# Second feed-forward matmul by half-block products: four of eight hidden groups with seven products instead of eight, in two passes

## The chip, the cores and the metric

The kernel runs on one core of one Trainium2 chip. The metric is device time in microseconds (us) of one execution; the times below are medians of several runs. Engines are named as in the profile: PE is TensorE's matmul (PEld its weight load), DVE is VectorE, ACT is ScalarE, POOL is GpSimd, SP issues the DMAs.

## The reference, cut to what matters

One layer of a streaming encoder on a sequence of 512 frames with 1024 channels. The change touches the last part of it alone, the second matmul of the feed-forward block:

```python
xn = modulate(rmsnorm(h, norm2_g[l]), sh2, sc2)
ff = jnp.square(jax.nn.relu(xn @ w_ff1[l])) @ w_ff2[l]     # (512 x 4096) @ (4096 x 1024)
h = h + g2[:, None, :] * ff
...
return rmsnorm(h, final_g)
```

All of it is float32 to about float32's precision. A matmul is made of three: each operand is split into a high part (rounded to the matmul's own 32-bit form, fp32r) and the low rest, and high x high, low x high and high x low are summed in PSUM (`mm3`, lines 116 to 119).

## The kernel before, in words

The first feed-forward matmul (w_ff1) computes the 4096 hidden channels in eight groups of 512, groups 1 to 7 by seven half-block products P1 to P7 instead of eight, so that scheme is already in use there (lines 1010 to 1030; its products are the rows named P). The squared-relu results stay in SBUF as sixteen tiles `hq[n, nh, th]` for group n: half nh of the group's 512 hidden channels, half th of the 512 frames, 128 x 512 elements each. Rows name them h.

The second matmul (w_ff2) then runs over 32 pieces k of 128 hidden rows. A piece is loaded on SP's queue (`raw_f`, 512 KB), ACT rounds it to its high part (`wh_f`, line 95), DVE subtracts to get the low part (`wl_f`, line 96); the hidden tiles are split in the same way on DVE (`hsh`, `hsl`, lines 1040 and 1041). Each piece is 24 matmuls of 128x128 by 128x512: four blocks of frames, two halves of the 1024 columns, three matmuls each, into eight PSUM banks `ob`. Up to three pieces are split ahead (the pools `raws` and `wpool` have three buffers each). The last four pieces (`LAST`) are split early and multiplied block by block, so that the gate, residual and final norm of one block run while the next is multiplied.

Each engine runs its instructions in the order in which they stand in the program, which a scheduler has set; a waiting instruction holds up all behind it on that engine. Tiles of a closed pool give their memory to the next pool, and what is written there waits for the last reader of the old tile.

Of the kernel before, what the change touches and what calls it, by code (L numbers as in the profile page):

```python
# [49 lines left out]
def block_kernel(ctx, tc, vecs_d, rows_d, ws_d, x_d, w_ada, w_in, w_out, w_ff1, w_ff2, out_d):  # L50
    nc = tc.nc
    act, dve, pool, pe, sp = nc.scalar, nc.vector, nc.gpsimd, nc.tensor, nc.sync

# [705 lines left out]
    for half in range(2):  # L759
        cs = slice(half * 512, (half + 1) * 512)  # L760
# [6 lines left out]
        for k in range(4 * half, 4 * half + 4):  # L767
# [75 lines left out]
    for k in range(KT):  # L843
# [169 lines left out]
    for n in range(1, NB):  # L1013
        c = {(nh, th): ring(f"h{n}{nh}{th}") for nh in range(2) for th in range(2)}
# [17 lines left out]
    ws_ff = Stream([(w_ff2[k * P:(k + 1) * P, :], 1, D, f"f2{k}") for k in range(FF // P - LAST)], 2)  # L1032
    ws_ff.prefetch(2)
    hsq = {}

    def hs_pair(kp, alloc):
        for th in range(2):
            src = hq[kp // 2, kp % 2, th]
            h_, l_ = alloc(th)
            dve.tensor_copy(out=h_, in_=src)  # L1040
            dve.tensor_sub(out=l_, in0=src, in1=h_.bitcast(F32))  # L1041
            hsq[kp, th] = (h_, l_)

    def hs_sc(th):
        hl = fp.tile([P, 2, 2, 256], F32R, tag="sc", name=f"hs0{th}", bufs=2)
        return hl[:, 0], hl[:, 1]

    hs_pair(0, hs_sc)
# [6 lines left out]
    o_banks = [[bank(f"ob{t}{hf}") for hf in range(2)] for t in range(TB)]  # L1055
    NK = FF // P

    def ff2_piece(k, last=False):
        if last:
            raw = raws.tile([P, 1, D], F32, tag="raw", name=f"raw_f2{k}")  # L1060
            sp.dma_start(out=raw[:, 0, :], in_=w_ff2[k * P:(k + 1) * P, :])
            wh = hsp.tile([P, 1, D], F32R, tag="lwh", name=f"wh_f2{k}", bufs=LAST)
# [5 lines left out]
        if k % 2 == 0 and k > 0:  # L1068
            hs_pair(k // 2, lambda th: [hsp.tile([P, 2, 256], F32R, tag="hs" + q, name=f"hs{q}{k}{th}", bufs=4)
                                        for q in "hl"])  # L1070
        return wh, wl

    def mm_f2(k, t, hf, wh, wl, stop):
        cs = slice(hf * 512, (hf + 1) * 512)
        h_, l_ = (v[:, k % 2, (t % 2) * P:(t % 2 + 1) * P] for v in hsq[k // 2, t // 2])
        mm3(o_banks[t][hf], h_, l_, wh[:, 0, cs], wl[:, 0, cs], k == 0, stop)

    for k in range(NK - LAST):
        wh, wl = ff2_piece(k)
# [80 lines left out]
```

## Time and profile before

| | |
|---|---|
| median of 3 runs | 819.65 us (819.43 to 820.51) |
| the profiled execution: its time, its span | 822.66 us, 820.1 us |
| PE busy in the span | 807.5 us (98%) |
| DVE, ACT busy | 554.4 us (68%), 359.4 us (44%) |
| second feed-forward matmul | about 637 to 812 us of the span |
| read from HBM | 104.44 MB |

Busy is the share of the span in which an engine had an instruction in work. The span is that of the profiled execution; its time is 2.6 us longer, and the runs without the profiler have a median 3.0 us below it. The page's second section has the granted clock of TensorE in tenths; it is at 9 in all slices of the second matmul.

### The profile page before, as it was taken

To read this page: it belongs to the slowest core of one execution; us is meant where nothing else is said; L and a number is where in the kernel's file an instruction comes from. 1 tells how busy PE (TensorE), PEld (TensorE's weight loads), DVE (VectorE), ACT (ScalarE), POOL (GpSimd) and SP (SyncE) were. 2 spreads that over 40 slices of the span, in tenths; PEclk is the share of its full clock that TensorE was granted. 3 is DMA by queue.
4 is the path that set the end of the run, shared out by engine and by line. 5 is a ranking of instruction groups with operands and counts; after the bars stand their busy time and mean duration, and the time that the engine had idled before them with its cause. 6 is when DMAs were issued, how large, how long until landed. Compare 5 with 4: busy or idle time off the path is not lost.

```text
span 820.1 us, 11377 instructions
## 1 busy us (share of the span) xinstructions
PE 807.5 (98%) x4423; PEld 700.8 (85%) x4423; DVE 554.4 (68%) x863; ACT 359.4 (44%) x540; POOL 43.1 (5%) x62
## 2 busy tenths in 40 slices
PE   8999999999999999999999999999999999999995
PEld 6887888888888888888888899999999888888884
DVE  4889767684834367988666689888888544444555
ACT  5457556274432333232444456666666311222213
POOL 2004020121100000100000000000000000000000
PEclk8999999999999999999999999999999999999998
DMA  8974331153233399577344241333321433223402
GB/s 254 268 229 119 116 104 47 27 136 96 78 103 94 110 330 293 169 247 271 108 170 159 83 126 51 104 106 109 116 83 54 152 103 103 83 98 103 129 0 103
DMA packets 66823, 107.28 MB, mean 131 GB/s; under 512 B 5329, under 2 KB 38225, under 8 KB 66769
## 3 DMA queue, kind: packets, MB, share of 16 engines
q1 hardware_dynamic: 66768, 106.56, 41.6%
q8 instruction: 34, 0.56, 0.3%
q14 instruction: 21, 0.16, 0.1%
HBM read 104.44 MB, written 2.10 MB: 130 GB/s over the span
## 4 chain that ended last, share of the span: by engine, by line
PE 93%; ACT 2%; DMA 1%; DVE 1%; issue 1%; POOL 0%; SPq 0%; POOLq 0%; DVEq 0%
PE ob L119 7%; PE ob L118 7%; PE ob L117 7%; PE P L118 6%; PE P L119 6%; PE P L117 6%; PE qk L282 4%; PE wo L117 1%; PE wo L119 1%; PE wo L118 1%; PE cp L241 1%; PE k1b L117 1%; PE gb0b L118 1%; PE q1b L118 1%; PE q1b L119 1%
## 5 line engine op out<-in xcount | busy, mean ns | idle before, releaser
L117 PE MATMUL ob<-wh_f,hsh 128*128 128x512 f32 x240 | 93.4, 389 | 0.0
L118 PE MATMUL ob<-wl_f,hsh 128*128 128x512 f32 x240 | 93.4, 389 | 0.0
L119 PE MATMUL ob<-wh_f,hsl 128*128 128x512 f32 x240 | 93.4, 389 | 0.0
L95 ACT CAST wh_f<-raw_f 128x1024 fp32r<-128x1024 f32 x28 | 29.6, 1056 | 110.6 <-PE ob L119 107.6
L96 DVE TENSOR_TENSOR wl_f<-raw_f,wh_f 128x1024 fp32r<-128x1024 f32 x28 | 34.3, 1225 | 55.7 <-ACT wh_f L95 54.7
L117 PEld LDWEIGHTS ob<-wh_f,hsh 128*128 128x128 f32 x240 | 45.1, 188 | 9.4
L118 PEld LDWEIGHTS ob<-wl_f,hsh 128*128 128x128 f32 x240 | 45.1, 188 | 9.4
L119 PEld LDWEIGHTS ob<-wh_f,hsl 128*128 128x128 f32 x240 | 45.1, 188 | 9.2
L921 ACT CAST wh_T<-T 128x1024 fp32r<-128x1024 f32 x21 | 22.0, 1049 | 22.8 <-PE P L118 21.1
L117 PE MATMUL P<-x2h,wh_B 128*128 128x256 f32 x112 | 31.6, 282 | 0.0
L118 PE MATMUL P<-x2l,wh_B 128*128 128x256 f32 x112 | 31.6, 282 | 0.0
L119 PE MATMUL P<-x2h,wl_B 128*128 128x256 f32 x112 | 31.6, 282 | 0.0
L1040 DVE CAST hsh<-h 128x512 fp32r<-128x512 f32 x30 | 12.7, 425 | 25.5 <-PE ob L118 25.5
L921 ACT CAST wh_B<-B 128x1024 fp32r<-128x1024 f32 x21 | 22.0, 1049 | 16.7 <-PE P L118 15.7
L922 DVE TENSOR_TENSOR wl_T<-T,wh_T 128x1024 fp32r<-128x1024 f32 x21 | 25.7, 1224 | 2.5 <-ACT wh_T L921 2.5
L922 DVE TENSOR_TENSOR wl_B<-B,wh_B 128x1024 fp32r<-128x1024 f32 x21 | 25.6, 1218 | 0.1
L96 DVE TENSOR_TENSOR wl_gb<-raw_gb,wh_gb 128x1024 fp32r<-128x1024 f32 x8 | 9.8, 1224 | 19.7 <-ACT wh_gb L95 19.6
L1041 DVE TENSOR_TENSOR hsl<-h,hsh 128x512 fp32r<-128x512 f32 x30 | 20.7, 692 | 2.6
L667 DVE SCALAR_TENSOR_TENSOR accg<-arg,c_act,accg 128x1024 f32<-128x1024 f32 x14 | 18.0, 1283 | 6.3 <-DMA arg<-in_w_ada 6.1
L118 PEld LDWEIGHTS P<-x2l,wh_B 128*128 128x128 f32 x112 | 21.3, 190 | 0.0
L117 PEld LDWEIGHTS P<-x2h,wh_B 128*128 128x128 f32 x112 | 21.3, 190 | 0.0
L119 PEld LDWEIGHTS P<-x2h,wl_B 128*128 128x128 f32 x112 | 21.3, 190 | 0.0
(548 smaller groups left out, 2491.8 us busy)
## 6 DMA issues: line engine op xcount, KB each, us to landing
raw_f<-in_w_ff SPq DMA_DIRECT2D x36, 512.0 KB, 3.3
B<-in_w_ff SPq DMA_DIRECT2D x28, 512.0 KB, 3.8
ar<-in_w_ada SPq DMA_DIRECT2D x64, 128.0 KB, 3.3
arg<-in_w_ada SPq DMA_DIRECT2D x16, 512.0 KB, 6.0
raw_o<-in_w_in SPq DMA_DIRECT2D x8, 512.0 KB, 3.8
raw_mv<-in_w_in SPq DMA_DIRECT2D x8, 512.0 KB, 3.6
raw_gb<-in_w_in SPq DMA_DIRECT2D x8, 512.0 KB, 3.7
raw_v<-in_w_in SPq DMA_DIRECT2D x8, 512.0 KB, 3.6
```

The source lines that it names most:

```text
L95: act.copy(out=wh, in_=raw)
L96: dve.tensor_sub(out=wl, in0=raw, in1=wh.bitcast(F32))
L117: pe.matmul(out, lhsT=ah, rhs=bh, start=start, stop=False)
L118: pe.matmul(out, lhsT=ah, rhs=bl, start=False, stop=False)
L119: pe.matmul(out, lhsT=al, rhs=bh, start=False, stop=stop)
L241: pe.matmul(cps[c][:, o:o + 1], lhsT=tile_[:, vi, f * P:(f + 1) * P], rhs=rhs, start=first and q == 0, stop=last and q == len(todo) - 1)
L282: pe.matmul(bk, lhsT=wx[:, kk, f * P:(f + 1) * P], rhs=xx[k], start=k == 0 and ps_ == 0, stop=k == KT - 1 and ps_ == 2)
L667: dve.scalar_tensor_tensor(out=acc, in0=raw, scalar=c_act[:, k:k + 1], in1=acc, op0=ALU.mult, op1=ALU.add)
L921: act.copy(out=wh, in_=src)
L922: dve.tensor_sub(out=wl, in0=src, in1=wh.bitcast(F32))
L1040: dve.tensor_copy(out=h_, in_=src)
L1041: dve.tensor_sub(out=l_, in0=src, in1=h_.bitcast(F32))
```

## The change

Of the eight hidden groups, six are done in a new way before the last two. A group of 512 hidden rows is a product of the 512 x 512 hidden values, in halves by frames and by hidden channels (a11, a12 for the first half of the frames, a21, a22 for the second), with 512 rows of w_ff2, in halves by rows and by columns (F11, F12, F21, F22 in the load's names, 512 KB each). A step is one product of half-blocks: 12 matmuls of 128x128 by 128x512 into two banks.

Groups 0, 1, 3 and 4 (W) take seven steps: P1 = a11 F11, P2 = a12 F21, P7 = (a11 - a21)(F22 - F12), P3 = (a12 - a21 - a22 + a11) F22, P5 = (a21 + a22)(F12 - F11), P6 = (a21 + a22 - a11)(F22 - F12 + F11) and P4 = a22 (F21 - F22 + F12 - F11). Groups 2 and 5 (S) take the plain eight steps, named P2, P3 (first pass) and P4, E (second pass). All groups add into the same banks g..., so eight banks would not hold seven products of two banks: the first pass runs P1, P2, P7, P3 over groups 0 to 5, the second P5, P6, P4 (and E) over the same groups with the weights loaded again. Between and after the passes DVE combines the banks into tiles r. Groups 6 and 7 (pieces k = 24 to 31) follow as before, and continue in the banks of P4 and E for the second half of the frames.

```diff
+    GROUPS = "WWSWWS"
...
+    left = Feed({0: (0, "F11"), 1: (0, "F21")}, order,
+                lambda nm: raws.tile([P, 2, 512], F32, tag="raw", name=nm), 3)
+    right = Feed({0: (1, "F12"), 1: (1, "F22")}, order,
+                 lambda nm: pass_pool[0].tile([P, 2, 512], F32, tag="q2", name=nm, bufs=4), 0)
...
+        if i % 5 < 3:
+            wh, wl = wtile("wh", f"wh_g{i}", 2, 512), wtile("wl", f"wl_g{i}", 2, 512)
+        else:
+            wh, wl = (pass_pool[0].tile([P, 2, 512], F32R, tag="wx" + q, name=f"w{q}_x{i}", bufs=2) for q in "hl")
+        act.copy(out=wh, in_=src)
+        dve.tensor_sub(out=wl, in0=src, in1=wh.bitcast(F32))
...
+        act.copy(out=h_, in_=src)
+        dve.tensor_sub(out=l_, in0=src, in1=h_.bitcast(F32))
...
+                if kind == "W" and pas == 0:
+                    yield hl(a11), w_pair(left.get(), left)
+                    yield hl(a12), w_pair(left.get(), left)
+                    b12, b22 = right.get(), right.get()
+                    s3 = fp.tile([P, 2, 256], F32, tag="tmp", name=f"S3{n}", bufs=2)
+                    dve.tensor_sub(out=s3, in0=a11, in1=a21)
+                    dve.tensor_sub(out=b12, in0=b22, in1=b12)
+                    yield hl(s3), w_pair(b12, right)
+                    dve.tensor_add(out=a21, in0=a21, in1=a22)
+                    dve.tensor_sub(out=a11, in0=a21, in1=a11)
+                    dve.tensor_sub(out=a12, in0=a12, in1=a11)
+                    yield hl(a12), w_pair(b22, right)
+                elif kind == "W":
+                    b11, b12 = left.get(), right.get()
+                    dve.tensor_sub(out=b12, in0=b12, in1=b11)
...
+                    yield hl(a21), w_pair(b12)
+                    b22 = right.get()
+                    dve.tensor_sub(out=b22, in0=b22, in1=b12)
...
+                    yield hl(a11), w_pair(b22)
+                    b21 = left.get()
+                    dve.tensor_sub(out=b21, in0=b21, in1=b22)
...
+                    yield hl(a22), w_pair(b21, left)
...
     x2s.close()
     mhs.close()
     hsp = ff.enter_context(tc.tile_pool(name="hsp", bufs=1, side="right"))
     fing = hsp.tile([P, D], F32, name="fing")
     sp.dma_start(out=fing, in_=rows_d[5].partition_broadcast(P))
+    ps_stack = ExitStack()
+    pass_pool.append(ps_stack.enter_context(tc.tile_pool(name="passes", bufs=1, side="right")))
+    for _ in range(4):
+        right.more()
...
+    for i, (pas, key) in enumerate(plan_):
+        prefetch_step(5)
+        (h_, l_), (wh, wl) = ready.pop(0)
...
+            for j in range(2):
+                mm3(acc_b[key, t], h_[:, j, ts_], l_[:, j, ts_], wh[:, j], wl[:, j], first and j == 0,
+                    i == last_of[key] and j == 1 and key not in ("P4", "E"))
...
+    ps_stack.close()
+    lwp = ff.enter_context(tc.tile_pool(name="lwp", bufs=1, side="right"))
```

The buffers of F12 and F22 (`q2`) and two of the five pairs of split weights (`wx`) lie in a pool on the memory that the first matmul's operands held; F11 and F21 use the buffers that `raw_f` had.

On SP's queue, where the first matmul ends (B are its last loads, raw_f the pieces of w_ff2, fing the final norm's row), there stood before:

```order
L916 DMA B710_5909<-in_w_ff1 128x4x256
L93 DMA raw_f20_6231<-in_w_ff2 128x1024
L916 DMA B711_5911<-in_w_ff1 128x4x256
L93 DMA raw_f21_6237<-in_w_ff2 128x1024
L93 DMA raw_f22_6264<-in_w_ff2 128x1024
```

Now there stands, from the second of the B loads on:

```order
L916 DMA B711_5911<-in_w_ff1 128x4x256
L1053 DMA F21022_6233<-in_w_ff2 128x2x512
L1053 DMA F11121_6235<-in_w_ff2 128x2x512
L1053 DMA F21120_6244<-in_w_ff2 128x2x512
L1053 DMA F12023_6265<-in_w_ff2 128x2x512
L1053 DMA F11219_6253<-in_w_ff2 128x2x512
L1147 DMA fing_6260<-in_rows 128x1024
L1053 DMA F22022_6267<-in_w_ff2 128x2x512
L1053 DMA F12121_6269<-in_w_ff2 128x2x512
L1053 DMA F22120_6271<-in_w_ff2 128x2x512
```

The third digit of an F name is its group: F22 of group 0 (F22022), the second load into the new pool, stands behind fing and a load for group 2.

On DVE around the last addition of the first matmul, h710 (h are hidden tiles, S and F sums and weights, hsl and wl the low parts), there stood before:

```order
L96 TENSOR_TENSOR wl_f20_6234<-raw_f20_6231,wh_f20_6233 128x1024
L1027 TENSOR_TENSOR h701_6015<-h701_6015,P47_6175 128x512
L96 TENSOR_TENSOR wl_f21_6240<-raw_f21_6237,wh_f21_6239 128x1024
L1029 TENSOR_TENSOR h710_6016<-h710_6016,P37_6203 128x512
L1040 CAST hsh20_6330<-h010_4529 128x512
L96 TENSOR_TENSOR wl_f22_6267<-raw_f22_6264,wh_f22_6266 128x1024
```

and now, seven operations behind h710:

```order
L1093 TENSOR_TENSOR hsl7_6351<-S31_6347,hsh7_6350 128x512
L1109 TENSOR_TENSOR h100_4596<-h101_4597,h100_4596 128x512
L1105 TENSOR_TENSOR S34_6619<-h400_5307,h401_5308 128x512
L1110 TENSOR_TENSOR h110_4598<-h110_4598,h100_4596 128x512
L1106 TENSOR_TENSOR F12023_6265<-F22022_6267,F12023_6265 128x1024
L1076 TENSOR_TENSOR wl_x3_6294<-F22022_6267,wh_x3_6293 128x1024
L1076 TENSOR_TENSOR wl_x4_6304<-F11121_6235,wh_x4_6303 128x1024
L1076 TENSOR_TENSOR wl_g2_6281<-F12023_6265,wh_g2_6280 128x1024
```

Behind h710 the next weight's split stood second before. Now ten operations of 128x512 stand there (the last four of them are shown), and F12023, the first that needs F22022, stands eleventh.

On PE the first 24 matmuls of the second matmul were those of piece 0, and piece 1 followed (ob are the banks, wh_f20 and wh_f21 the high parts of the two pieces):

```order
L119 MATMUL ob30_6262<-wh_f20_6233,hs01_6246 128x512
L117 MATMUL ob31_6263<-wh_f20_6233,hs01_6246 128x512
L118 MATMUL ob31_6263<-wl_f20_6234,hs01_6246 128x512
L119 MATMUL ob31_6263<-wh_f20_6233,hs01_6246 128x512
L117 MATMUL ob00_6256<-wh_f21_6239,hs00_6243 128x512
L118 MATMUL ob00_6256<-wl_f21_6240,hs00_6243 128x512
```

Now P1 and P2 of group 0 take the place of piece 0, and from the last matmul of P2 on there stands (gP1, gP2, gP3, gP7 are the banks; wh_g2 is the high part of F22 - F12, wh_x3 of F22, wh_x4 of the next group's F11):

```order
L119 MATMUL gP21_6340<-wh_g1_6249,hs01_6246 128x512
L117 MATMUL gP10_6309<-wh_x4_6303,hsh5_6299 128x512
L117 MATMUL gP11_6316<-wh_x4_6303,hsh5_6299 128x512
L117 MATMUL gP70_6360<-wh_g2_6280,hsh3_6276 128x512
L117 MATMUL gP71_6367<-wh_g2_6280,hsh3_6276 128x512
L117 MATMUL gP30_6387<-wh_x3_6293,hsh4_6289 128x512
L118 MATMUL gP30_6387<-wl_x3_6294,hsh4_6289 128x512
L119 MATMUL gP30_6387<-wh_x3_6293,hsl4_6290 128x512
L117 MATMUL gP30_6387<-wh_x3_6293,hsh4_6289 128x512
L118 MATMUL gP30_6387<-wl_x3_6294,hsh4_6289 128x512
L119 MATMUL gP30_6387<-wh_x3_6293,hsl4_6290 128x512
L118 MATMUL gP70_6360<-wl_g2_6281,hsh3_6276 128x512
```

Two matmuls of group 1 were put ahead of P7 and P3 of group 0; P7's low part, wl_g2, is wanted eight matmuls after P7's first. In all PE has 4295 rows in place of 4343.

## Rows read from the trace of the kernel before

**Rows 1.** The page: the span, its first section (busy us, share, instructions), and the head of the chain that ended last, by engine.

```profile
span 820.1 us, 11377 instructions
PE 807.5 (98%) x4423; PEld 700.8 (85%) x4423; DVE 554.4 (68%) x863; ACT 359.4 (44%) x540; POOL 43.1 (5%) x62
PE 93%; ACT 2%; DMA 1%; DVE 1%; issue 1%; POOL 0%; SPq 0%; POOLq 0%; DVEq 0%
```

**Rows 2.** All waits of PE in the whole span, by what it waited for: us in total, times, longest us.

```profile
PE xt L321 <- POOL epsc L307: 2.5, 1, 2.5
PE xt L315 <- DVE xt L333: 1.3, 2, 0.8
PE k1b L117 <- ACT wh_k L95: 0.2, 1, 0.2
```

**Rows 3.** Busy us (and instructions) of each engine in stretches, granted clock, DMA share, GB/s: one of the first matmul's, its crossing to the second, one of the second.

```profile
600.00:620.00 20.00, 20.00 (x171) 20.00 (x171) 17.34 (x19) 12.91 (x17) 0.00 (x0) 1.00 0.25 79
637.00:660.00 23.00, 23.00 (x106) 19.12 (x105) 11.17 (x18) 5.93 (x7) 0.00 (x0) 1.00 0.43 138
660.00:700.00 40.00, 40.00 (x178) 33.15 (x177) 16.96 (x21) 7.89 (x8) 0.00 (x0) 1.00 0.28 93
```

**Rows 4.** The matmuls of the second matmul: duration ns min/median/max, first and last start us. The first row is of pieces 0 and 1, the other of the rest.

```profile
L117 PE MATMUL ob<-wh_f,hs x16: 389/389/396, 637.5 to 647.7; 128*128 128x512 f32 x16
L119 PE MATMUL ob<-wh_f,hsl x240: 388/389/389, 648.8 to 811.3; 128*128 128x512 f32 x120
```

**Rows 5.** PE in order of time at the crossing: start us, us, instruction.

```profile
637.34 0.28 PE L119 MATMUL P<-S4hl,wl_B 128*128 128x256 f32 x1
637.46 0.40 PE L117 MATMUL ob<-wh_f,hs 128*128 128x512 f32 x1
```

**Rows 6.** DVE in order of time, in the first matmul and at its crossing to the second (in brackets: idle before it, what ended that).

```profile
522.18 1.23 DVE L922 TENSOR_TENSOR wl_T<-B,wh_T 128x1024 fp32r<-128x1024 f32 x1 [1.46 <-ACT wh_T L921]
570.65 1.22 DVE L922 TENSOR_TENSOR wl_B<-B,wh_B 128x1024 fp32r<-128x1024 f32 x1
571.78 1.22 DVE L943 TENSOR_TENSOR T<-B,T 128x1024 f32<-128x1024 f32 x1
572.92 0.68 DVE L1024 TENSOR_TENSOR h<-h,P 128x512 f32<-128x512 f32 x1
573.52 0.68 DVE L1025 TENSOR_TENSOR h<-h,P 128x512 f32<-128x512 f32 x1
574.12 1.22 DVE L922 TENSOR_TENSOR wl_B<-B,wh_B 128x1024 fp32r<-128x1024 f32 x1
637.66 0.69 DVE L1029 TENSOR_TENSOR h<-h,P 128x512 f32<-128x512 f32 x1 [0.65 <-PE P L119]
649.65 1.23 DVE L96 TENSOR_TENSOR wl_f<-raw_f,wh_f 128x1024 fp32r<-128x1024 f32 x1 [4.21 <-ACT wh_f L95]
```

**Rows 7.** ACT in order of time: a 128x512 cast with what follows it, and 128x1024 casts at the crossing.

```profile
497.41 0.62 ACT L989 CAST S1hl<-xn 128x512 fp32r<-128x512 f32 x1
497.93 0.59 ACT L976 ACTIVATE h<-f10b 128x512 f32<-128x512 f32 x1
634.70 1.05 ACT L95 CAST wh_f<-raw_f 128x1024 fp32r<-128x1024 f32 x1 [0.59 <-PE P L118]
635.65 0.63 ACT L976 ACTIVATE h<-h 128x512 f32<-128x512 f32 x1
```

**Rows 8.** SP's queue at the crossing in order of time, and from the page the DMA issues (KB each, median us to landing).

```profile
634.43 2.94 SPq L93 DMA_DIRECT2D raw_f<-in_w_ff  x2
637.65 0.67 SPq L1053 DMA_DIRECT2D fing<-in_rows  x1
639.87 5.92 SPq L93 DMA_DIRECT2D raw_f<-in_w_ff  x2
...
fing<-in_rows SPq DMA_DIRECT2D x1, 512.0 KB, 5.7
```

**Rows 9.** The same table for the six microseconds after the crossing and two of the single ones in them (last two columns: DMA share, GB/s), and for one loaded stretch.

```profile
638.00:644.00 6.00, 6.00 (x28) 4.98 (x27) 5.35 (x10) 2.63 (x4) 0.00 (x0) 1.00 0.80 261
641.00:642.00 1.00, 1.00 (x6) 0.83 (x5) 1.00 (x3) 0.00 (x0) 0.00 (x0) 1.00 0.74 201
643.00:644.00 1.00, 1.00 (x6) 0.84 (x5) 0.38 (x1) 0.88 (x1) 0.00 (x0) 1.00 0.28 115
290.00:295.00 5.00, 5.00 (x24) 4.14 (x23) 1.43 (x2) 1.06 (x1) 0.52 (x1) 1.00 1.00 374
```

**Rows 10.** The granted clock (third column from the right, 1.00 is 2.4 GHz, 0.50 is 1.2 GHz) at the start of the kernel and after its last matmul, as stretches.

```profile
14.00:15.00 1.00, 1.00 (x12) 1.00 (x10) 0.96 (x3) 0.74 (x2) 0.00 (x0) 0.98 0.88 165
15.00:18.30 3.30, 3.30 (x14) 3.01 (x14) 2.27 (x9) 2.10 (x4) 0.00 (x0) 0.50 0.90 254
18.30:21.80 3.50, 3.50 (x10) 2.73 (x9) 3.43 (x12) 2.15 (x6) 0.00 (x0) 0.50 0.92 272
21.80:23.00 1.20, 1.20 (x8) 1.01 (x8) 0.84 (x2) 1.18 (x3) 0.00 (x0) 1.00 0.88 247
...
811.00:812.00 1.00, 0.73 (x4) 0.26 (x2) 0.43 (x2) 0.30 (x2) 0.00 (x0) 1.00 1.03 383
813.50:813.75 0.25, 0.00 (x0) 0.00 (x0) 0.25 (x1) 0.25 (x1) 0.00 (x0) 0.86 0.00 0
813.75:814.00 0.25, 0.00 (x0) 0.00 (x0) 0.19 (x2) 0.19 (x2) 0.00 (x0) 0.50 0.00 0
```

More of the change, by code (lines that the diff above doesn't have):

```diff
@@ L1030, in block_kernel @@
         relu2(c12, c12)
[L1032 to L1046, printed above, removed]
@@ L1048, in block_kernel, with later, __init__, more @@
-    hs_pair(0, hs_sc)
+    GROUPS = "WWSWWS"
+    NF = len(GROUPS)
+    NK = FF // P
+    KF = 4 * NF
+    def later(kind, pas):
+        return {("W", 0): ("P1", "P2", "P7", "P3"), ("W", 1): ("P5", "P6", "P4"),
+                ("S", 0): ("P2", "P3", "P2", "P3"), ("S", 1): ("P4", "E", "P4", "E")}[kind, pas]
+    class Feed:
+        def __init__(self, cols, order, make, ahead):
+            self.todo = [(n, kh, cols[kh]) for n in order for kh in range(2)]
+            self.make, self.have = make, []
+            for _ in range(ahead):
+                self.more()
+        def more(self):
+            if self.todo:
+                n, kh, (jh, nm) = self.todo.pop(0)
+                raw = self.make(f"{nm}{n}{len(self.todo)}")
+                r0 = n * 512 + kh_rows[nm] * 256
+                sp.dma_start(out=raw, in_=w_ff2[r0:r0 + 256, jh * 512:(jh + 1) * 512].rearrange("(k p) c -> p k c", p=P))
+                self.have.append(raw)
+        def get(self):
+            return self.have.pop(0)
@@ new lines, in block_kernel, with w_pair @@
+    kh_rows = {"F11": 0, "F21": 1, "F12": 0, "F22": 1}
+    order = list(range(NF)) * 2
+    left = Feed({0: (0, "F11"), 1: (0, "F21")}, order,
+                lambda nm: raws.tile([P, 2, 512], F32, tag="raw", name=nm), 3)
+    right = Feed({0: (1, "F12"), 1: (1, "F22")}, order,
+                 lambda nm: pass_pool[0].tile([P, 2, 512], F32, tag="q2", name=nm, bufs=4), 0)
+    pass_pool = []
+    count = [0, 0]
+    def w_pair(src, feed=None):
+        i = count[0]
+        count[0] += 1
+        if i % 5 < 3:
[4 more added lines that the diff above has]
+        dve.tensor_sub(out=wl, in0=src, in1=wh.bitcast(F32))
+        if feed:
+            feed.more()
+        return wh, wl
@@ L1049, in block_kernel, with prefetch_step @@
+    plan_ = [(pas, key) for pas in range(2) for kind in GROUPS for key in later(kind, pas)]
+    gen = passes()
+    ready = []
+    def prefetch_step(m):
+        while len(ready) < m:
+            s_ = next(gen, None)
+            if s_ is None:
+                return
+            ready.append(s_)
+    prefetch_step(2)
     x2s.close()
@@ new lines, in block_kernel, with rtile, gated, after @@
+    acc_b, res = {}, {}
+    def rtile(nm, t):
+        res[nm, t] = hsp.tile([P, 512], F32, name=f"r{nm}{t}")
+        return res[nm, t]
+    def gated(nm, t, row, hf):
+        cs = slice(hf * 512, (hf + 1) * 512)
+        r_ = res[nm, t]
+        dve.tensor_mul(out=r_, in0=r_, in1=g2[:, cs])
+        dve.tensor_add(out=xr[:, row, cs], in0=xr[:, row, cs], in1=r_)
+    def after(key):
+        for t in range(2):
+            b_ = acc_b.get((key, t))
+            if key == "P1":
+                act.copy(out=rtile("1", t), in_=b_)
+            elif key == "P7":
+                dve.tensor_add(out=rtile("7", t), in0=res["1", t], in1=b_)
+            elif key == "P3":
+                dve.tensor_add(out=rtile("3", t), in0=res["1", t], in1=b_)
+            elif key == "P2":
+                dve.tensor_add(out=res["1", t], in0=res["1", t], in1=b_)
+            elif key == "P6":
+                dve.tensor_add(out=res["3", t], in0=res["3", t], in1=b_)
+                dve.tensor_add(out=res["7", t], in0=res["7", t], in1=b_)
+            elif key == "P5":
+                dve.tensor_add(out=res["3", t], in0=res["3", t], in1=b_)
+                dve.tensor_add(out=rtile("5", t), in0=res["7", t], in1=b_)
@@ L1058, in ff2_piece @@
+    ps_stack.close()
+    lwp = ff.enter_context(tc.tile_pool(name="lwp", bufs=1, side="right"))
+    o_banks = [[bank(f"ob{t}{hf}") for hf in range(2)] for t in range(2)]
+    o_banks += [[acc_b["P4", t], acc_b["E", t]] for t in range(2)]
+    late = [(nm, t, row + t, hf) for nm, row, hf in (("3", 0, 1), ("7", 2, 0), ("5", 2, 1)) for t in range(2)]
     def ff2_piece(k, last=False):
@@ L1067, in ff2_piece @@
             wh, wl = ws_ff.next()
-        if k % 2 == 0 and k > 0:
-            hs_pair(k // 2, lambda th: [hsp.tile([P, 2, 256], F32R, tag="hs" + q, name=f"hs{q}{k}{th}", bufs=4)
-                                        for q in "hl"])
+        if k % 2 == 0 and k > KF:
+            hs_pair(k // 2)
         return wh, wl
@@ L1075, in mm_f2 @@
         h_, l_ = (v[:, k % 2, (t % 2) * P:(t % 2 + 1) * P] for v in hsq[k // 2, t // 2])
-        mm3(o_banks[t][hf], h_, l_, wh[:, 0, cs], wl[:, 0, cs], k == 0, stop)
-    for k in range(NK - LAST):
+        mm3(o_banks[t][hf], h_, l_, wh[:, 0, cs], wl[:, 0, cs], k == KF and t < 2, stop)
+    for k in range(KF, NK - LAST):
         wh, wl = ff2_piece(k)
@@ L1082, in block_kernel @@
                 mm_f2(k, t, hf, wh, wl, False)
+        for _ in range(2):
+            if late:
+                gated(*late.pop(0))
     pcs = [ff2_piece(k, True) for k in range(NK - LAST, NK)]
```

55 lines of the change are left out of this document (51 added, 4 removed).

## The prediction

> **What bounds the kernel now.** I read the page first: PE is busy for 98% of the span, and the chain that ended last is PE for 93% [rows 1]. Then the waits of PE: three rows in all, each of transposes or of an early projection, and none that names a weight or a hidden tile of the feed-forward block [rows 2]. So the second feed-forward matmul is PE at its own pace. Its 768 matmuls (32 pieces of 24) start between 637.46 us and 811.3 us [rows 4, 5], 173.8 us over 767 steps, 0.2267 us each (the 389 ns of a row [rows 4] overlap one another). Last, the stretch table, for what could take PE's place: DVE is busy for 16.96 of 40 us in the second matmul, ACT for 7.89, DMA for a share of 0.28, all at full clock [rows 3]. In the first matmul, which already uses seven products, DVE stands at 17.34 of 20 us and PE still doesn't wait [rows 3].
>
> **What the change removes.** Four groups go from 8 to 7 steps of 12 matmuls: 48 matmuls less, the same number by which the order of PE shrinks. 48 × 0.2267 = 10.88 us. A step lasts 12 × 0.2267 = 2.72 us, so four steps 10.88 us and the three steps of a W group in the second pass 8.16 us.
>
> **What it adds on DVE and ACT, pass by pass.** Behind each other, DVE operations start 1.13 us apart at 128x1024 (570.65, 571.78, 572.92) and 0.60 us apart at 128x512, operands in PSUM included (572.92, 573.52, 574.12) [rows 6]; I use 1.135 and 0.60. W in the first pass: four weight splits and a weight sum (5 × 1.135), four hidden splits and four hidden sums (8 × 0.60), 10.5 us of 10.88. W in the second pass: three splits and three sums of weights, three hidden splits, 6 × 1.135 + 3 × 0.60 = 8.6 us of 8.16, so 0.45 short. S: 4 × 1.135 + 2 × 0.60 = 5.7 us of 10.88, 5.1 to spare. ACT needs 0.95 + 0.52 us per step [rows 7], 1.5 of 2.72. The folds between the passes put eight additions (4.8 us) on DVE within the first two W groups of the second pass, so DVE falls behind there by up to 4.8 + 2 × 0.45 = 5.7 us. What hides it is the lead: there are five pairs of split weights, so DVE can be four steps (10.9 us) ahead, less a cast and a split (2.1 us), 8.8. The S group that follows gives 5.1 us back, the next two W groups take 0.9, and the last folds (eight additions) fall in the second S. I put this at **0**; without the lead it would cost the 5.7. Groups 6 and 7 have twelve additions and multiplications for the gates, 7.2 us, in 16 steps of which DVE now uses 42% [rows 3]: also 0. A few sums for group 0 and later move ahead into the first matmul; DVE has gaps there such as the 1.46 us at 522 us [rows 6], and I put 0.1 us for one that meets none; at most two operations, 1.2 us.
>
> **What it adds on the queue.** Groups 0 to 5 are loaded twice, 24 loads of 0.524 MB more. The first pass needs 2.1 MB per 10.88 us (193 GB/s), a W group of the second 2.1 MB per 8.16 us (257 GB/s). The kernel has moved 374 GB/s over 5 us [rows 9]. I put the loads at **0**; the other bound is a rival below.
>
> **The entry, where a new wait stands.** PE does P1 and P2 of group 0 from 637.46, 24 × 0.2267, and is through at 642.9. Next it wants F22 − F12 of group 0. F22 lies in the new pool, whose memory comes free with the last product of the first matmul at 637.3 to 637.7 [rows 5]. On SP it stands behind a load for group 2 and fing: of the two loads at 634.43 that took 2.94 us to issue the second leaves at about 637.1, fing at 637.65 with 0.67 [rows 8], so F22 is issued at about 638.3. How long it is under way: fing, the same size beside others, took 5.7 us [rows 8], and the 6 us from 638 moved 1.57 MB (261 GB/s), three loads, with the rate falling from 201 to 115 by 643 [rows 9], so three are in at about 643.5. I take 643.8 (642.5 to 646). Meanwhile DVE does ten half operations behind h710, which starts at 637.66 with 0.69 [rows 6]: 638.35 + 10 × 0.60 = 644.35. Then the weight sum (645.5). ACT casts wh_x3, wh_x4 and wh_g2 in this order, 0.95 apart [rows 7]: the third follows the sum and is there at 646.85. PE has only the two matmuls of P1 of group 1 between (0.45 us, at about 645.9, when wh_x4 is there). So it goes on at 646.9: 646.9 − 642.9 − 0.45 = 3.55 us lost. Eight matmuls on (648.7) it wants wl_g2; DVE has wl_x3 and wl_x4 before it, 1.135 each, and ends wl_g2 at 648.9: 0.2 more. Together **3.8 us**. An earlier load doesn't help by more than 0.2, since DVE isn't free before 644.35; a load that lands at 646 makes it 5.8. Everything behind on PE simply moves by this amount.
>
> **What the stall does to the clock.** From about 643.1 (the last matmul's end) to 645.9 PE has no matmul, 2.8 us, then two, then 0.6 us none. After the kernel's last matmul, ended at 811.73, the granted clock held 1.00 at first and was at 0.50 by 813.75, in a slice that averages 0.86 [rows 10]: it fell at 813.7, 2.0 us after PE fell idle. By that row it falls to half (1.2 GHz) here too, before the matmuls come back. How long it then stays isn't shown for a gap in the middle; the nearest rows are the start, 0.50 from 15.0 to 21.8 with few matmuls [rows 10]. At half the clock each us costs half a us. The bounds are 0 and 6.8 / 2 = 3.4; I take the middle, **1.7 us**, since PE is fully loaded at once when it comes back, where at the start it was not. The Trainium skill, "TensorE: Matmul & The Clock Gate", section "HAM oscillation — how this bites in real kernels", tells of kernels whose matmuls wait for a DMA between bursts and come back at the half clock; it speaks against this change, the trace shows no such gap in the second matmul, and the fall at 813.7 agrees with it. By it the sum below is −5.3, and if it didn't hold for one gap of this length, −7.0.
>
> **The sum.** −10.88 + 0.1 + 3.8 + 1.7 = −5.3 us on the profiled span, 820.1 to 814.8. The profiled execution took 822.66 us, the runs' median is 819.65, 3.0 below; the same step from the median gives **814.4 us**. The stretch behind the last matmul I leave as it is.
>
> **Rivals.** *The clock holds through the gap.* The row at 811 to 814 speaks against it, the two matmuls in the middle of the gap for it. −7.0 us, 812.6.
> *DVE becomes the bound in the second pass.* If its operations there don't overlap each other's ends but take their full 1.23 and 0.69 us [rows 6], a W group takes 6 × 1.23 + 3 × 0.69 = 9.45 us against 8.16: four groups fall 5.2 short and the eight fold additions 5.5 more; of these the S between gives back some 4.6 and the lead covers the rest only in part, as it is itself smaller after the entry. About 5 us: 819.3, no change that could be measured. Against it: the first matmul runs DVE at 87% with no wait of PE [rows 2, 3].
> *The loads bind; slower than before.* The first pass draws 193 GB/s and the second 257 GB/s in its W groups, each with at most seven loads ahead, whose buffers come free late. For it: the stretch at the entry reached only 261 GB/s with three loads in flight [rows 9], and two issues of loads take 2.94 us of SP [rows 8], about 1.5 each, so that four per W group take 6 of 8.16 us. Against it: 374 GB/s with more in flight [rows 9]. The saving left, 5.3 us, is gone when the four W groups of the second pass take 8.16 + 5.3 / 4 = 9.5 us each, 221 GB/s; at 200 GB/s they take 10.5 us, 9.4 us in all, and the time is 823.8.
> That the products stay as many is no rival: PE's order has the 48 less.
>
> **How the numbers follow.** The forecast 0.50, the clock that holds 0.28, DVE as bound 0.13, the loads 0.09. The first two span 811.6 (the clock holds, and a us less at the entry if some of the ten half operations are earlier) to 816.5 (the load lands at 646). The range reaches to DVE's case and leaves the loads out: 811.6 to 819.0. A difference of 0.2% (1.6 us) is about what a measurement of this kernel can tell from no change. Faster by more than that, below 818.0: the first two cases and a part of DVE's, 0.82. Same: most of DVE's and a piece of the loads', 0.10. Slower, above 821.3: 0.08.
>
> **What the profile after would show.** PE with 720 matmuls in the second matmul, 0.2267 us apart but for one gap; a wait at about 643 of some 3.5 us that names wh_x4 or wh_g2 (ACT) or F12023's sum, and a short one on wl_g2; the granted clock at 0.50 for some us behind it. DVE at 85 to 90% between 650 and 760 us with no other wait of PE, DMA at 190 to 260 GB/s. Wrong it would be if waits on wl or wh of the second pass stand in PE's list (DVE), if these end with DMAs of F tiles (loads), if the entry's wait is under 2 or over 6 us, or if matmuls in the middle of the passes stand further apart than 0.2267 us.

## The result and the profile after

The changed kernel takes 815.73 us (median; 813.60 to 816.33) against 819.54 us before: a ratio of 0.9941, 95% interval 0.9926 to 0.9956. It is 3.8 us faster by the medians; the forecast was 814.4, 5.3 us less than before. The profiled execution took 815.62 us with a span of 813.8.

The page's first rows, to be read beside [rows 1], and all waits of PE, beside [rows 2] (us in total, times, longest):

```profile
span 813.8 us, 11472 instructions
PE 795.4 (98%) x4375; PEld 689.1 (85%) x4375; DVE 615.3 (76%) x925; ACT 404.1 (50%) x606; POOL 43.0 (5%) x62
PE 93%; DMA 2%; SPq 1%; ACT 1%; issue 1%; DVE 1%; POOLq 0%; POOL 0%
...
PE gP L117 <- ACT wh_x L1075: 4.8, 1, 4.8
PE xt L321 <- POOL epsc L307: 2.5, 1, 2.5
PE xt L315 <- DVE xt L333: 2.3, 2, 1.5
PE gates L288 <- ACT xs L366: 0.7, 1, 0.7
PE qk L282 <- ACT xs L369: 0.3, 1, 0.3
PE k1b L117 <- ACT wh_k L95: 0.2, 1, 0.2
PE gP L117 <- ACT wh_g L1075: 0.2, 1, 0.2
```

There are 48 matmuls less. Two waits are new in the second matmul (the rows of gP), both at its entry, and none stands in the two passes behind it. The waits on gates and qk and the longer one on xt lie in the first 60 us of the span, which the change doesn't touch; the first two are missing again in other runs below (e1 to e8). PE around the entry, in order of time (start us, us; x2 is two matmuls joined in one row; in brackets the idle time before and what ended it), and the kernel's last matmul:

```profile
636.16 0.40 PE L117 MATMUL gP<-wh_g,hs 128*128 128x512 f32 x1
...
641.40 0.39 PE L119 MATMUL gP<-wh_g,hs 128*128 128x512 f32 x1
646.55 0.77 PE L117 MATMUL gP<-wh_x,hsh 128*128 128x512 f32 x2 [4.76 <-ACT wh_x L1075]
647.50 1.22 PE L117 MATMUL gP<-wh_g,hsh 128*128 128x512 f32 x2 [0.17 <-ACT wh_g L1075]
648.52 0.63 PE L117 MATMUL gP<-wh_x,hsh 128*128 128x512 f32 x1
...
650.60 0.40 PE L119 MATMUL gP<-wh_x,hsl 128*128 128x512 f32 x1
...
806.10 0.39 PE L119 MATMUL gE<-wh_f,hsl 128*128 128x512 f32 x1
```

From the first start to the last, 169.94 us go by; 719 steps of 0.2267 are 163.0. So 6.9 us are lost, all of it between 641.40 and 650.60. Two parts of it can be told apart. P2 is through at 641.63, two matmuls of the next group take 0.45, and P7's first starts at 647.50 instead of 642.08: 5.4 us of waiting. From there to 650.60 seven steps take 3.1 us in place of 1.6: 1.5 us of low clock. The second matmul is thus 10.88 - 6.94 = 3.94 us shorter than the 173.88 us of before [rows 4, 5], as the medians say (3.8). The forecast for it was -10.88 + 3.8 + 1.7 = -5.4 us.

The two spans differ by more, 6.3 us. The rest lies where the change has no part: the second matmul starts 1.3 us earlier (636.16 against 637.46 [rows 5]), and behind its last start stand 7.7 us instead of 8.7, though the kernel's last operations of ACT and DVE start 3.45 us behind it in both. Among all the profiled executions here that first start lies anywhere from 635.17 to 637.46. So kernels are compared below by the length of the second matmul from first to last start, less 0.2267 us per step; that is called the loss.

What ended the wait, on DVE, ACT and SP in order of time, and fing's transfer (KB, us from issue to landing):

```profile
642.44 0.69 DVE L1110 TENSOR_TENSOR h<-h,h 128x512 f32<-128x512 f32 x1
644.58 1.22 DVE L1106 TENSOR_TENSOR F<-F,F 128x1024 f32<-128x1024 f32 x1 [1.45 <-DMA F<-in_w_ff]
...
644.51 1.99 ACT L1075 CAST wh_x<-F 128x1024 fp32r<-128x1024 f32 x2 [4.39 <-DMA F<-in_w_ff]
646.41 1.99 ACT L1075 CAST wh_g<-F 128x1024 fp32r<-128x1024 f32 x2
...
636.36 0.84 SPq L1147 DMA_DIRECT2D fing<-in_rows  x1
637.25 0.94 SPq L1053 DMA_DIRECT2D F<-in_w_ff  x2
...
fing<-in_rows SPq DMA_DIRECT2D x1, 512.0 KB, 6.8
```

One load ahead of these, F12 of group 0 (its issue, and us from issue to landing):

```profile
L1053 SPq DMA_DIRECT2D F<-in_w_ff x1: 368/368/368, 633.9 to 633.9; - x1
DMA to landing us min/median/max: 5.3/5.3/5.3
```

PE's list names ACT, but ACT itself and DVE had been idle for 4.39 and 1.45 us, and a DMA ended both: F22 of group 0, issued at 637.25, lands at 644.5. fing lands at 636.36 + 6.8 = 643.2, so F22 comes 1.3 us behind it. F12 lands at 639.2 and the load for group 2, issued at 635.74, at 640.5. Of these issues fing's waits 0.2 us for the first matmul's last product on PE; F22's waits for nothing, SP only reaches it behind fing.

The clock at its fall and its rise (third column from the right), and PE (first after the length), DVE (third) and the GB/s (last) in the two passes, beside [rows 3]:

```profile
646.80:647.00 0.20, 0.20 (x2) 0.05 (x1) 0.20 (x2) 0.20 (x1) 0.00 (x0) 1.00 0.00 0
647.00:647.20 0.20, 0.20 (x2) 0.00 (x0) 0.20 (x1) 0.20 (x1) 0.00 (x0) 0.77 0.00 0
650.40:650.60 0.20, 0.20 (x2) 0.16 (x1) 0.20 (x1) 0.00 (x0) 0.00 (x0) 0.69 0.69 205
650.60:650.80 0.20, 0.20 (x2) 0.19 (x1) 0.20 (x1) 0.00 (x0) 0.00 (x0) 1.00 1.07 317
...
660.00:700.00 40.00, 40.00 (x178) 33.14 (x177) 35.17 (x40) 23.17 (x30) 0.00 (x0) 1.00 0.64 210
700.00:740.00 40.00, 40.00 (x178) 33.12 (x177) 38.60 (x45) 21.56 (x26) 0.00 (x0) 1.00 0.69 219
```

The clock was at 0.50 (1.2 GHz) from 647.1 to 650.5, 3.4 us. This is one execution: its mean granted clock is 0.994, that of the three other runs 0.990, so more of their time stood at 0.50; where is not recorded. (In the kernel before, the last slice of the clock on the page, which reaches into the second matmul, reads 8 and not 9; that is the fall at 813.7, behind the last matmul [rows 10].) In the passes DVE went from 42% to 88% and 96%, and PE keeps its 178 matmuls per 40 us, as many as before.

### The profile page after: what moved, and what is told of

It is laid out like the page before. It is cut to its first block, busy times and chain, and to the rows that moved or that the text cites. A ratio compares the mean times of both kernels' runs of the same rounds, so it can differ in the third digit from the quotient of the medians.

```text
span 813.8 us, 11472 instructions
## 1 busy us (share of the span) xinstructions
PE 795.4 (98%) x4375; PEld 689.1 (85%) x4375; DVE 615.3 (76%) x925; ACT 404.1 (50%) x606; POOL 43.0 (5%) x62
## 4 chain that ended last, share of the span: by engine, by line
PE 93%; DMA 2%; SPq 1%; ACT 1%; issue 1%; DVE 1%; POOLq 0%; POOL 0%
PE P L119 6%; PE P L117 6%; PE P L118 6%; PE gP L117 5%; PE gP L118 5%; PE gP L119 5%; PE qk L282 4%; PE wo L117 2%; PE wo L119 2%; PE wo L118 2%; PE f10b L118 1%; PE f10b L117 1%; PE f10b L119 1%; PE k1b L117 1%; PE o0b L119 1%
## 5 line engine op out<-in xcount | busy, mean ns | idle before, releaser
L1092 ACT CAST hsh<-h 128x512 fp32r<-128x512 f32 x38 | 23.6, 621 | 35.3 <-PE gP L118 27.2
L117 PE MATMUL gP<-wh_g,hsh 128*128 128x512 f32 x92 | 36.2, 396 | 0.2 <-ACT wh_g L1075 0.2
L118 PE MATMUL gP<-wl_g,hsh 128*128 128x512 f32 x92 | 35.8, 389 | 0.0
L119 PE MATMUL gP<-wh_g,hsl 128*128 128x512 f32 x92 | 35.8, 389 | 0.0
L1075 ACT CAST wh_g<-F 128x1024 fp32r<-128x1024 f32 x27 | 28.2, 1049 | 13.7 <-issue 7.1
L1076 DVE TENSOR_TENSOR wl_g<-F,wh_g 128x1024 fp32r<-128x1024 f32 x27 | 32.9, 1222 | 2.6 <-ACT wh_g L1075 2.5
L117 PE MATMUL gP<-wh_x,hsh 128*128 128x512 f32 x60 | 23.8, 400 | 4.8 <-ACT wh_x L1075 4.8
L118 PE MATMUL gP<-wl_x,hsh 128*128 128x512 f32 x60 | 23.7, 396 | 0.0
L119 PE MATMUL gP<-wh_x,hsl 128*128 128x512 f32 x60 | 23.6, 393 | 0.0
L1076 DVE TENSOR_TENSOR wl_x<-F,wh_x 128x1024 fp32r<-128x1024 f32 x17 | 20.7, 1222 | 1.4 <-ACT wh_x L1075 1.4
```

Of the source, the lines that this page charges most:

```text
L1075: act.copy(out=wh, in_=src)
L1076: dve.tensor_sub(out=wl, in0=src, in1=wh.bitcast(F32))
L1092: act.copy(out=h_, in_=src)
```

## Experiments

All edits are made to the changed kernel.

### The next group's plain products put ahead (e1)

```diff
+                    for m in {0: (0, 1), 1: ()}.get(n, (n,)):
+                        yield hl(hq[m, 0, 0]), w_pair(left.get(), left)
+                        yield hl(hq[m, 1, 0]), w_pair(left.get(), left)
...
+    plan_[2:6] = [(0, k_) for k_ in ("P1", "P2", "P7", "P3")]
```

> P1 and P2 of group 1 stand ahead of P7 and P3 of group 0: 48 matmuls instead of 24 before the first that needs F22 (10.9 us instead of 5.4). In the changed kernel the wait and the low clock cost 6.9 us by the trace (the eleventh matmul after P2 starts 9.2 us after P2's last, where 2.3 would do). Theory, the entry alone costs this: PE's wait at the entry falls to 1 us or less (on wl of F22 - F12, which DVE would have at about 648.5), the clock stays at 1.00, and the time falls by about 6 us, to 809.8. Rival, the loads are what PE waits for over the whole first pass and the wait only moves: PE waits as long some steps later, time within 1.5 us of the changed kernel's 815.7.

Measured: 809.31 us, ratio to before 0.9868 (0.9855 to 0.9882). Of the loss 0.7 us is left, around one wait (PE in order of time):

```profile
647.13 0.50 PE L118 MATMUL gP<-wl_x,hsh 128*128 128x512 f32 x1 [0.43 <-DVE wl_x L1076]
```

F22's way is about the same here (the sum starts at 642.97, 7.8 us after the second matmul's first start, where it was 8.4, and a DMA ended the idle time before it), but it is covered. The entry alone was the loss, and it doesn't come back later.

### F22 issued first (e2)

```diff
-    sp.dma_start(out=fing, in_=rows_d[5].partition_broadcast(P))
...
-    for _ in range(4):
+    for _ in range(2):
+        right.more()
+    left.more()
+    for _ in range(2):
         right.more()
...
-        if feed:
+        if feed and i != 0:
             feed.more()
...
         if i == end0 + 6:
+            sp.dma_start(out=fing, in_=rows_d[5].partition_broadcast(P))
```

> F22 of group 0 is issued ahead of the load for group 2, and the final norm's row is loaded in the second pass; DVE then has five operations of group 1 and 3 behind the weight sum instead of ahead of it. Theory, the load sets the end of the wait, since three transfers stand ahead of it on a queue that is at 350 to 418 GB/s: F22 lands at about 641 instead of 644.5, the high part of F22 - F12 is there at about 644 instead of 647.5, PE loses about 3 us less, 812.5. Rival, the load takes its 7 us wherever it stands, since all loads in flight share the rate: it lands 1.5 us earlier at most, and the gain is under 1.6 us.

Measured: 811.59 us, 0.9897 (0.9883 to 0.9910). PE and ACT in order of time, two stretches with the clock, and F22's load (issue, and us to landing):

```profile
642.61 0.39 PE L119 MATMUL gP<-wh_g,hs 128*128 128x512 f32 x1
644.31 0.73 PE L117 MATMUL gP<-wh_x,hsh 128*128 128x512 f32 x2 [1.31 <-ACT wh_x L1075]
645.26 0.73 PE L117 MATMUL gP<-wh_g,hsh 128*128 128x512 f32 x2 [0.22 <-ACT wh_g L1075]
...
642.26 1.99 ACT L1075 CAST wh_x<-F 128x1024 fp32r<-128x1024 f32 x2 [0.95 <-DMA F<-in_w_ff]
...
643.00:644.00 1.00, 0.00 (x0) 0.00 (x0) 1.00 (x2) 1.00 (x2) 0.00 (x0) 1.00 1.04 389
646.00:647.00 1.00, 1.00 (x6) 0.77 (x5) 1.00 (x2) 0.16 (x1) 0.00 (x0) 1.00 0.91 303
...
L1053 SPq DMA_DIRECT2D F<-in_w_ff x1: 462/462/462, 635.5 to 635.5; - x1
DMA to landing us min/median/max: 6.7/6.7/6.7
```

F22 is there 4.9 us after the second matmul's start (637.37 here), where it took 8.35 in the changed kernel (644.51 against 636.16): 3.4 us earlier, against the rival's 1.5. Most of that is the issue: it goes out at 635.52, 1.85 us before the second matmul's start, so its memory was free by then, and in the changed kernel only the order on SP held it back until 1.1 us after the start. On the way it is for 6.7 us, against 7.2, near the 7 us of the rival. The loss is 2.15 us (802.52 - 637.37 - 163.0), 4.8 less; 1.5 us of that is the clock, which stayed at 1.00. My expectation had not counted on it.

### The wait filled with idle matmuls (e3)

```diff
+                if i == 2:
+                    d_h, d_w = used[0]
+                    for q_ in range(11):
+                        pe.matmul(acc_b[key, t], lhsT=d_h[:, q_ % 2, 0:P], rhs=d_w[:, q_ % 2], start=True, stop=True)
```

> 22 matmuls that compute nothing that is used (group 0's P1 operands into P7's banks, overwritten later) stand on PE behind P2, 5.0 us of work in the wait. The wait's end is not touched: the high part of F22 - F12 comes at about 647.5. Theory, the low clock costs about 1.5 us of the 6.9 by itself (0.50 from 647.2 to 650.4): with PE busy in the gap it stays at 1.00, ten matmuls go at 0.227 instead of 0.4 us, and as the two matmuls of the next group no longer fill the wait 0.45 us are given back: time 1 us lower, 814.7. Rival, the clock falls all the same or its loss lies within the wait: no difference, or 0.5 us more.

Measured: 814.72 us, 0.9933 (0.9920 to 0.9945), an interval that holds the changed kernel's 0.9941 too: the time decides nothing. The trace does (PE and the clock):

```profile
641.39 4.47 PE L1208 MATMUL gP<-wh_g,hs 128*128 128x512 f32 x19
647.10 0.50 PE L117 MATMUL gP<-wh_g,hsh 128*128 128x512 f32 x1 [1.24 <-ACT wh_g L1075]
647.43 0.86 PE L1208 MATMUL gP<-wh_g,hs 128*128 128x512 f32 x3
...
646.00:647.00 1.00, 0.00 (x0) 0.00 (x0) 1.00 (x2) 1.00 (x3) 0.00 (x0) 1.00 0.04 14
648.00:650.00 2.00, 2.00 (x11) 1.62 (x10) 2.00 (x3) 0.52 (x1) 0.00 (x0) 1.00 0.92 268
```

With PE busy for most of the gap the clock doesn't fall, and the steps behind it are at full pace. From first to last start it takes 169.55 us against 169.94: behind P7's first start 0.1 us is lost instead of 1.5, so the clock's share is back, but three of the added matmuls fell behind P7's first (0.7 us) and the two of the next group no longer fill the wait (0.45). I had counted only the second of these.

### Five groups by seven products (e4)

```diff
-    GROUPS = "WWSWWS"
+    GROUPS = "WWWWWS"
```

> Five groups by seven products and one plain (the plain one in the middle becomes one of seven): 12 matmuls less, 2.72 us, and DVE and loads have no plain group to catch up before the last. Theory of the prediction, the lead of DVE hides it: behind by 4.8 us of folds and 5 x 0.45 us, 7.0 in all, less than the lead of 8.8: no wait of PE in the second pass, 2.7 us faster than the changed kernel, 813.0. Rival, DVE binds in the second pass: PE waits on low parts there, some 2 to 5 us, 813 to 816 or more. Rival, loads bind (257 GB/s over 41 us): waits that end with loads, each W group over 8.16 us.

Measured: 812.17 us, 0.9903 (0.9888 to 0.9918). The second matmul takes 167.04 us from first to last start, 2.9 less than in the changed kernel, 2.72 of it the twelve matmuls. Behind the entry PE waits for nothing (a stretch of 100 us, columns as above):

```profile
660.00:760.00 100.00, 100.00 (x443) 82.84 (x442) 98.40 (x117) 56.03 (x71) 0.00 (x0) 1.00 0.59 191
```

DVE is at 98% and still not the bound; nor are the loads. At the entry the same wait (4.0 us) had the clock at 0.50 from 644.0 to 650.8 here, twice as long, half of it while PE waited anyway; the loss is 6.8 us, hardly other than 6.9.

### Three pairs of split weights in place of five (e5)

On e1's order:

```diff
-        if i % 5 < 3:
+        if True:
             wh, wl = wtile("wh", f"wh_g{i}", 2, 512), wtile("wl", f"wl_g{i}", 2, 512)
...
-        prefetch_step(5)
+        prefetch_step(3)
```

> The order of e1 (P1 and P2 of two groups first), but three pairs of split weights instead of five, so that splits are at most two steps ahead of the matmuls. Theory, what hides DVE's shortage in the second pass is this lead: the prediction's ledger has DVE behind by up to 5.7 us there, and two steps less a cast and a split leave 5.4 - 2.1 = 3.3: PE waits on low parts in the second pass, 2.4 us in all, 811.7 against 809.3 of e1. Rival, DVE has room enough and the lead hides nothing: no wait of PE in the second pass and 809.3 within 0.8.

Measured: 809.52 us, 0.9859 (0.9832 to 0.9886), as e1. In the second pass a wait does stand now, which e1 has not (PE, then DVE):

```profile
732.78 0.50 PE L118 MATMUL gP<-wl_g,hsh 128*128 128x512 f32 x1 [0.23 <-DVE wl_g L1076]
...
698.15 1.23 DVE L1115 TENSOR_TENSOR F<-F,F 128x1024 f32<-128x1024 f32 x1 [0.77 <-DMA F<-in_w_ff]
727.12 1.23 DVE L1115 TENSOR_TENSOR F<-F,F 128x1024 f32<-128x1024 f32 x1 [0.48 <-DMA F<-in_w_ff]
730.37 1.23 DVE L1119 TENSOR_TENSOR F<-F,F 128x1024 f32<-128x1024 f32 x1 [0.28 <-DMA F<-in_w_ff]
```

Added up over the starts of the matmuls between 729 and 736, 0.9 us are lost there, not the 2.4 that I expected. Nor does this stand where the ledger has DVE short, in the first two W groups of the second pass (702 to 718 us here, by the count of matmuls): there nothing is lost. It stands in the third W group, and ahead of it DVE itself sat idle for loads, 0.48 and 0.28 us. So it isn't the ledger's shortage, and how much of that the lead hides in the changed kernel is not shown.

### Both entry edits, and five groups by seven products (e6)

The edits of e1 and e2, and with them:

```diff
-    GROUPS = "WWSWWS"
+    GROUPS = "WWWWWS"
```

> e1's order, e2's loads (F22 ahead of the load for group 2 and of the final norm's row) and e4's five groups by seven products in one kernel. If the three causes are apart from each other, the entry costs nothing more (e1 has 0.7 us left of it) and the 12 matmuls give 2.7 us: 809.3 - 0.7 - 2.7 = 805.9. If DVE has no lead to spare now that PE arrives 6 us earlier, waits on low parts take a part of it: 807 to 809.

Measured: 806.83 us, 0.9831 (0.9805 to 0.9857), 0.9 us above the 805.9 that the three would give if they simply added up. The entry is free of loss, and one new wait stands at the start of the second pass:

```profile
709.50 0.50 PE L117 MATMUL gP<-wh_g,hsh 128*128 128x512 f32 x1 [0.98 <-DVE r L1183]
...
708.75 1.29 DVE L1183 TENSOR_TENSOR r<-r,gP 128x512 f32<-128x512 f32 x2
```

PE wants the bank that this addition reads. It isn't a weight that is late but a fold, which stands on DVE behind the splits made ahead.

### The final norm's row loaded later (e7)

```diff
-    sp.dma_start(out=fing, in_=rows_d[5].partition_broadcast(P))
...
         if i == end0 + 6:
+            sp.dma_start(out=fing, in_=rows_d[5].partition_broadcast(P))
```

The scheduler put it on the queue right behind F22, F12 and F22 of groups 0 and 1.

> The changed kernel with one edit: the final norm's row is no longer loaded ahead of F22 of group 0 but behind it and the two loads after. In the changed kernel this row's transfer lands 2.7 us behind the one before it, the weight loads 1.3 us apart. Theory, this one transfer is what the prediction's landing time left out: F22 lands at about 641.8 instead of 644.5, the high part of F22 - F12 comes at about 644.7, the gap without a matmul is about 2 us and the clock stays at 1.00 as in e2; PE loses 2.6 instead of 6.9 us, 811.4. Rival, the queue is full whatever stands on it and F22 lands 1.3 us earlier at most: 1 to 2 us gained, 814.

Measured: 813.55 us, 0.9910 (0.9886 to 0.9934). ACT, PE, the clock, and F22's load (issue, and us to landing):

```profile
642.54 1.99 ACT L1075 CAST wh_x<-F 128x1024 fp32r<-128x1024 f32 x2 [2.04 <-DMA F<-in_w_ff]
...
644.59 0.73 PE L117 MATMUL gP<-wh_x,hsh 128*128 128x512 f32 x2 [2.41 <-ACT wh_x L1075]
645.54 1.22 PE L117 MATMUL gP<-wh_g,hsh 128*128 128x512 f32 x2 [0.22 <-ACT wh_g L1075]
...
646.00:648.60 2.60, 2.60 (x7) 2.02 (x7) 2.60 (x4) 0.43 (x1) 0.00 (x0) 0.50 0.80 262
...
L1053 SPq DMA_DIRECT2D F<-in_w_ff x1: 1322/1322/1322, 636.5 to 636.5; - x1
DMA to landing us min/median/max: 6.0/6.0/6.0
```

F22 is there 6.0 us after the second matmul's start (642.54 against 636.55) instead of 8.35, 2.35 earlier. Of that 1.1 us is the issue, which no longer stands behind fing's (at the second matmul's start here, 1.1 behind it in the changed kernel), and the rest the way, 6.0 us against 7.2. So as a transfer fing cost about what a weight load does. The 2.6 us that it lands behind the load ahead of it in the changed kernel are the most of five executions: in e1, e3, e4 and e5, where it stands at the same place, these are 1.3 to 1.8 us. The other half of the theory fell: the clock did go to 0.50, behind a wait of 2.4 us, where e2's wait of 1.3 us left it alone. Each is one trace, though: of e7's six runs one (811.42 us) has a mean clock of 0.996, the others 0.988 to 0.993. By an estimate 0.996 leaves at most 7.3 us at 0.50. In each trace here the kernel's start takes 3.4 us of that or more and its end 2.4 or more, so in that run hardly anything is left for the entry and the clock probably held there. The loss is 4.8 us (804.32 - 636.55 - 163.0), 2.2 less than in the changed kernel, and the time 2.2 us lower.

### Both entry edits alone (e8), and e6 with the fold put earlier (e9)

The first kernel has e1's and e2's edits together, the second is e6 with this:

```diff
-    for i_, keys in ((last_of["P7"] + 2, ("P1", "P7")), (end0 + 2, ("P3", "P2")),
+    for i_, keys in ((last_of["P7"] + 2, ("P1", "P7")), (end0, ("P3", "P2")),
```

> e1's order and e2's loads on the groups of the changed kernel (four by seven products). If the entry is all that the change lost, the second matmul is now 719 steps of 0.2267 us and nothing else: 0.7 us below e1 (809.3), 808.6, with no wait of PE behind 636 us and the saving of 10.9 us whole. If DVE, which no longer gains time on PE in a wait at the entry, is the next bound, a wait of 0.5 us or more appears behind 690 us.

> e6 with the folds of P3's and P2's banks put on DVE two steps earlier. In e6 PE waits 1.0 us at 709.5 for a bank that DVE reads (L1183) at 708.75 to 709.4, behind eight operations that prepare later steps, though P3's last product is done some microseconds before. Theory, only the place of the fold is wrong and DVE keeps up with the weights: the wait goes and PE has none behind 636 us, 1.2 us less, 805.6. Rival, DVE has no time left (it is busy for all of 660 to 740 us in e6): the wait moves to a low part, 806.8 or more.

Measured: 807.78 us, 0.9847 (0.9833 to 0.9860), for the first; 806.21 us, 0.9820 (0.9805 to 0.9834), for the second, the fastest here. Neither has a wait of PE in the second matmul. From first to last start the first takes 163.01 us (635.21 to 798.22), the second 160.28 (636.34 to 796.62), which are 719 and 707 steps of 0.2267 to a few hundredths. By the times e6 and the second can't be told apart, as their intervals overlap; by the traces the loss goes from 1.3 us to nothing. The second kernel, over 100 us:

```profile
660.00:760.00 100.00, 100.00 (x443) 82.81 (x442) 100.00 (x121) 56.13 (x73) 0.00 (x0) 1.00 0.61 195
```

DVE has no idle time in these 100 us and PE doesn't wait. The saving of the change, 10.9 us, is whole in the first kernel (173.88 - 163.01); what it had lost was the entry. By the medians the first kernel is 12.85 us below the kernel before, measured again beside it (820.63), 2.0 more than its matmuls account for; for the changed kernel and the other edits the medians give from 0.1 us less to 1.4 us more than the matmuls do. All ten profiled executions with the change have 7.7 us behind the last start where the one before has 8.7, which may be a part of it; the rest is not explained.

## Why the prediction was right, and where it was off

**The matmuls.** 48 × 0.2267 = 10.88 us: the pace holds in all stretches without a wait, and e8 has the whole amount.

**The entry's wait** was sized at 3.8 us and is 5.4. The step that failed is F22's time under way. DVE's part was right: its ten half operations end at 643.0, 6.9 us after the second matmul's start (the prediction had 644.35, 6.9 after 637.46). F22's issue at 637.25 is 1.1 after that start (0.8 forecast), though not because its memory came free so late: e2 issues it 1.85 us before the start. But the load was taken as under way for 5.5 us, by fing and by a stretch of three loads, and took 7.2, so that it landed 8.35 us after the start instead of 6.3. The three loads counted were the one for group 2, fing and F22. F12 of group 0, in at 639.2, was under way too, so four had to land, on a queue at 350 to 430 GB/s where F22 and the two behind it land 1.3 us apart. The runs bear the count out: counted from F12, F22 is the fourth transfer in the changed kernel, e1, e3, e4 and e5 and lands 7.6 to 8.3 us after the start; the third in e7, 6.0 us; the second in e2, e6 and e8, 4.8 to 5.2 us. So e7's theory, that fing was what the landing time left out, was wrong: fing had been counted. The prediction's sentence that an earlier load helps by no more than 0.2 rested on DVE as the later of the two; with the load later, it was the load that counted (e2). The 0.2 us for wl_g2 didn't come: at half the clock PE reached it later.

**The clock** was sized at 1.7 us and cost 1.5. It fell at 647.1, not 2.0 us after PE fell idle as behind the kernel's last matmul [rows 10] but 5.3 us after, when the matmuls had come back; in e4 it fell 2.3 us after, in the middle of the wait. So the size was near by luck, a middle between far bounds, and the moment wrong. In the traces the clock held behind e2's wait of 1.3 us and fell behind e7's of 2.4. The Trainium skill, "TensorE: Matmul & The Clock Gate", section "HAM oscillation — how this bites in real kernels", tells of this kind of loss, a wait for a DMA and then matmuls at half the rate, there at each step of a loop. This case's traces agree in kind, with 1.5 us for one such gap.

**DVE at nothing** was right, and by more than the ledger said. DVE was at 88 and 96% and PE didn't wait; with a fifth group by seven products 98%, and in e9 100%. The ledger's 5.7 us of shortage in the first two W groups of the second pass is too much: with two of five pairs taken away nothing was lost there, where I expected 2.4 us (e5). One step of it that the rows contradict is that all of DVE's work is tied to the pairs of split weights. A weight sum needs none, only loaded tiles: in e5 the second group's first sum starts at 698.15, 12 us ahead of its product on PE (710.2), where the pairs allow two steps, 5.4 us. How much of the 5.7 this explains stays open. Where DVE did hold up PE in the end, in e6, it was by a fold that freed a bank, which the ledger had counted as work but not as something that PE waits for.

**The loads at nothing** was right in the passes: 210 to 219 GB/s and no wait of PE there that ends with a transfer. DVE sat idle for a load twice (0.75 us at 668.9, 0.52 us at 718.2), which its lead covered. At the entry it was wrong, as told. An argument for the rival had no ground: the 2.94 us of two issues [rows 8] run from the start of the first to the end of the second, with SP idle between; one issue of these loads takes 0.37 us (median of the 48), not about 1.5.

**The 0.1 us of moved operations** can't be seen: the first start of the second matmul differs by more than a microsecond between profiled executions, and is already 1.2 us earlier in this one at the first matmuls of w_ff1 (471.9 against 473.1), ahead of any moved operation.

The rivals of DVE and of the loads as bounds of the passes did not come true; that of the clock that holds did so only where the gap was shorter (e1, e2) or filled (e3).

## What to carry to other kernels

A load goes out only behind all that stands ahead of it on its queue, so one that has to wait for memory (here fing) holds back another whose memory is free (F22); and the work at a crossing should be work whose operands are already there: two more steps on plain operands hid 6.2 of the 6.9 us (e1), and with the loads put in a better order all of it (e8). When such a load is priced, count every transfer that is still under way when it goes out, and not only those issued with it. An engine at 100% need not be the bound, but then it is the place of what it frees in its order that counts.

## What was not expected of the hardware

Loads of 512 KB issued within a few microseconds of each other did not land together but one behind the other: in the changed kernel F22 1.3 us behind fing, the two after it 1.3 us apart. So one such load took from 4.8 to 8.3 us from the second matmul's start to be there, by the number of transfers ahead of it. A row broadcast to 128 partitions, also listed with 512 KB, landed 1.3 to 1.8 us behind the load ahead of it in four executions and 2.6 us in a fifth; what makes the difference is not shown. Half the clock stayed for 3.4 us after one wait of 4.8 us and for 6.8 us after a wait of 4.0 us, and both cost PE about the same, since half of the longer one lay in the wait.
